# Decay rows of a token mixer: spread over the partitions by DMAs from DRAM instead of one-hot matrix products

## The chip, the cores and the metric

The kernel runs on one core of one Trainium2 chip. The metric is the device time of one launch in microseconds. The kernel before takes 2029.32 us (median of 3 runs, 2028.66 to 2029.45).

## What is computed

A decoder trunk of two layers on 512 tokens of width 1024. Each layer is a gated feed-forward block, a mixer, and a second feed-forward block. The mixer runs three kinds of heads side by side on one input projection: 4 mLSTM heads, 4 retention heads and 4 gated-delta heads, and one output projection merges them. Cut to what the change touches:

```python
bcum = jnp.cumsum(fc, axis=-1)                                   # mLSTM, per head
log_w = jnp.where(causal, bcum[..., :, None] - bcum[..., None, :] + ic[..., None, :], -jnp.inf)
m_row = jnp.maximum(log_inter, jnp.max(log_w, axis=-1))
w = jnp.exp(log_w - m_row[..., None])
...
g = jnp.cumsum(ac, axis=-1)                                      # gated delta, per head
diff = g[..., :, None] - g[..., None, :]
decay = jnp.where(causal, jnp.exp(jnp.where(causal, diff, 0.0)), 0.0)
...
o = (q * exp(g)) @ S + ((q @ k.T) * decay) @ u
...
x = x + concat(y_mlstm, y_retention, y_delta) @ w_out
```

So each of the 4 mLSTM heads and 4 delta heads has one row of 512 numbers (a running maximum, or a running sum of log decays, one number a token) that must stand in all 128 partitions: it is the term that varies along the free axis, while the other varies along the partitions.

## The kernel before

Activations lie with features on the partitions and the 512 tokens along the free axis. Each weight tile of 128x1024 is split into a high and a low part (`wh`, `wl`), and each product of 128x128 by 128x512 is made of three (`mm3`). In a mixer the input projection is 32 weight tiles of 24 products each (`pin`, in `dense_tok` `ptok`), then 8 tiles of the output projection (`po_`). The raw weights are loaded by SP's queue. The low part is made in a mixer by ScalarE (`wl` <- minus the raw tile) and a DMA of the GpSimd queue that loads the raw tile a second time and adds it (`w_split`, L299).

The small work of the heads is written as generators (`gate_math` L874, `decays` L1049, `delta_inverse` L1077, `q_post` L1208, `mlstm` L1363, and others). While the program is built, `dense_mm` and the output projection call `poll()` (L836) after each three products; it runs the next piece of a generator if a planner (`Clock`, L103) believes that its inputs are there (`mark`/`wait`) and that its engines are not too far behind (`STEPS` names the engines of each piece). So the planner's times set where each small instruction stands between the dense products. Each engine then runs its instructions in that order, whatever the true times are. `until(...)` (L850) lets the planner's time pass until a key is marked; nothing dense is put on TensorE meanwhile.

The names that matter: `prow` (rows transposed into PSUM), `RB` (the 8 rows as a high and a low part on partitions 0 to 7 and 32 to 39), `SEL` (one-hot columns), `pG` and `pM` (a row in all partitions, in PSUM), `X` and `L` (decays and products of the delta inverse), `PT` (decays times scores for the delta output), `w` (for an mLSTM pair: decays `Es`, state, scaled queries), `pP` (delta scores q k), `po` (delta output, four blocks of 128 tokens), `vb` (that output, normalised), `py` (its transposes), `g`, `yh`, `yl` (the gated result and its two parts, the right side of `po_`). The tail of a mixer runs in this sequence: `q_post` of four heads, `chain_out` (L1297, `po`), `chain_norm` (L1313, four times a reduction and a chain of small vector instructions), `merge_delta` (L1531, `py`, `g`, `yh`, `yl`). The output projection's first two tiles need only the mLSTM and retention results (48 products with `ym` and `yr`). From the third on it needs all four token blocks of the delta result (`OUT_KEYS`, L31).

Every instruction is issued from the wrapper's line L182, so the rows of the profile are told apart by their tiles.

Of the kernel before, what the change touches and what calls it, by code (L numbers as in the profile page):

```python
# [9 lines left out]
F32 = mybir.dt.float32  # L10
# [17 lines left out]
BACKLOG = 1.65  # L28
VFIRST = 0.3
WARM = 11  # L30
OUT_KEYS = [("s0",), ("s1",), ("s2",), ("s3",)] + 4 * [("s4", "s5", "s6", "s7")]  # L31
# [12 lines left out]
    gate_act="A".split(),  # L44
    gate_math="V A V VG V V A V V A".split(),
    head_norm="c V c V V G".split(),
# [3 lines left out]
    norm_cols="V A".split(),  # L50
    q_post="A VA A VG".split(),
    retention="VG Vc c".split(),
# [11 lines left out]

C_ID, C_TRI, C_ONE, C_MT, C_MS, C_M32, C_COS, C_SIN, C_HALF, C_SEL, C_DEC, C_QD, C_KD, C_GC, C_SUM, C_END = (
    0, 128, 256, 260, 388, 516, 580, 708, 836, 838, 846, 1358, 1614, 1618, 1620, 1636)

# [5 lines left out]
def const_table():  # L73
# [13 lines left out]
    c[:, C_HALF + 1] = r % 2 == 1  # L87
    for j in range(8):
        c[j, C_SEL + j] = c[32 + j, C_SEL + j] = 1.0

# [77 lines left out]
def trunk(ctx, tc, a, out):  # L168
# [100 lines left out]
    Z4 = cst.tile([4, 1], F32, name="Z4")  # L269
    SEL = cst.tile([P, 8], F32, name="SEL")  # L270
    RB = cst.tile([P, S], F32, name="RB")
    zero = cst.tile([P, 1], F32, name="zero")

# [494 lines left out]
    def mixer(l, n, nxt, after):  # L768
# [93 lines left out]

        def bcast_row(ps, j):
            m = ps.shape[0]
            T.matmul(ps, r(SEL[:, j:j + 1].broadcast_to([P, m])), r(RB), start=True, stop=True)

# [7 lines left out]
        def gate_math():  # L874
# [72 lines left out]
            for t in range(NT):  # L947
                T.transpose(prow[0:8, t * P:(t + 1) * P], ag3[:, t, :], ident)
            row = tm[6][0:8, 0:S]
            V.tensor_copy(row, prow[0:8, :])  # L950
            V.tensor_tensor_scan(row[0:4, :], Z4.broadcast_to([4, S]), prow[0:4, :], 0.0, ALU.add, ALU.max)
            yield
            A.copy(r(RB[0:8, :]), row)
            yield
            V.tensor_sub(r(RB[32:40, :]), row, RB[0:8, :])
            env.update(bg3=bg3, ag3=ag3, ng3=ng3, bt=bt)
            mark("rows")
            yield
# [3 lines left out]
            flo = COL("flo", 16)  # L962
            V.tensor_tensor(v3(flo, 4), v3(pmc[:, 0:16], 4), bg3[:, :, 0:4], ALU.add)
            yield
            A.activation(flo, flo, AF.Exp, scale=-1.0)
# [83 lines left out]
        def decays():  # L1049

            yield from wait("rows")
            bg3 = env["bg3"]
            for hd in range(4):
                pG = SM("pG")
                bcast_row(pG, 4 + hd)
                E = X[:, hd, :]
                V.tensor_tensor(v3(E, P), bc4(maskS), v3(pG, P), ALU.subtract)
                V.tensor_copy(gl[:, hd * 4:hd * 4 + 4], v3(pG, P)[:, :, P - 1])
                yield
                for t in range(NT):  # L1060
                    s = slice(t * P, (t + 1) * P)
                    A.activation(E[:, s], E[:, s], AF.Exp, bias=bg3[:, t, 4 + hd:5 + hd])
                if hd == 3:
                    mark("decays")
                yield
            bght = bg3[:, :, 4:8].rearrange("p t h -> p h t")
            V.tensor_tensor(v3(kdec, 4), v3(gl, 4), bght, ALU.subtract)
            yield
            A.activation(kdec, kdec, AF.Exp)
            A.activation(eglast, gl, AF.Exp)  # L1070
            eg = COL("eg", 16)
            A.activation(v3(eg, 4), bght, AF.Exp)
            env["eg"] = eg
            mark("eg")
            yield
# [132 lines left out]
        def q_post(hd, kT, qT, odd):  # L1208
# [9 lines left out]
            V.tensor_reduce(ssq[:, hd * 4:hd * 4 + 4], v3(PT[:, hd, :], P), AX.X, ALU.add)  # L1218
            pG = SM("pG")
            bcast_row(pG, 4 + hd)  # L1220
            V.tensor_tensor(v3(PT[:, hd, :], P), v3(pG, P), bc4(maskT), ALU.add)
            A.activation(eG, pG, AF.Exp)
            yield
# [139 lines left out]
        def mlstm(pair, mqk, V1):  # L1363
# [6 lines left out]
            for b in range(2):  # L1370
                pM = SM("pM")
                bcast_row(pM, h0 + b)
                V.tensor_tensor(v3(Es[b], P), bc4(maskT), v3(pM, P), ALU.subtract)
                hb = slice(64 * b, 64 * b + 64)
                V.tensor_copy(mc[:, 4 * b:4 * b + 4], v3(pM, P)[:, :, P - 1])
                V.tensor_copy(mp[hb, :], mc[hb, 4 * b:4 * b + 4])
                V.tensor_tensor(v3(qs[hb, :], P), bc(mp[hb, 0:3], P), v3(pM[hb, :], P)[:, 1:4, :], ALU.subtract)
                yield
                for t in range(NT):
                    c = slice(t * P, (t + 1) * P)  # L1380
                    A.activation(Es[b][:, c], Es[b][:, c], AF.Exp, bias=ag3[:, t, h0 + b:h0 + b + 1])
                yield
# [338 lines left out]
    G.memset(Z4, 0.0)  # L1721
    G.memset(zero, 0.0)
    sqs = {}
# [23 lines left out]
    n.todo += [step for p in range(4) for step in n.sums(p)]  # L1747
    n.todo.append(lambda: (A.copy(r(SEL), C[:, C_SEL:C_SEL + 8]), A.copy(r(RB), zero.broadcast_to([P, S]))))
    for l in range(DEPTH):
# [75 lines left out]
```

## Time and profile before

| | |
|---|---|
| time, median of 3 runs | 2029.32 us |
| the profiled execution's own time | 2026.25 us |
| its span, from the first to the last instruction | 2024.5 us |
| mean granted TensorE clock | 0.996 of full speed |
| busy share of PE, DVE, ACT, POOL | 98%, 70%, 53%, 13% |
| mixers in the span, about | 368 to 666 us and 1365 to 1662 us |

Times below are from the profiled execution, in us from the start of its span. TensorE (PE) is in order, and a matmul's duration there contains an overlap with the next, so what a matmul costs is the distance from one start to the next. Idle time of an engine other than PE costs nothing unless PE waits for its result.

### The profile page before, as it was taken

Reading aid. Unit: us, or ns where it says so; the run is one execution under the profiler, and the core shown is the slowest. Engines: PE = TensorE matmul, PEld = TensorE weight load, DVE = VectorE, ACT = ScalarE, POOL = GpSimd, SP = SyncE. Lnnn points to the kernel's source line nnn. Section 1 sums busy time; section 2 is a strip of 40 time slices with the busy share of each in tenths; the row PEclk is TensorE's granted clock in tenths of the full one; section 3 lists DMA queues with packets and bytes.
Section 4 is the critical chain, followed back from the end, with each engine's and each line's share of the span. In section 5 each row is a group of like instructions: output and inputs, shape, how many; then the busy total and the mean of one; then the engine's idle time right before and its main releaser. Section 6 shows DMA issues by size and latency. Waiting matters only on the chain.

```text
span 2024.5 us, 32377 instructions
## 1 busy us (share of the span) xinstructions
PE 1992.9 (98%) x12865; PEld 1765.9 (87%) x12865; DVE 1412.9 (70%) x2447; ACT 1077.3 (53%) x1607; POOL 268.9 (13%) x311
## 2 busy tenths in 40 slices
PE   9999999999999999999999999999999999999997
PEld 6999988787888899998889998877878889999886
DVE  6888934568676788883588887335777758888623
ACT  5666622564476566662365555227545756655521
POOL 0000001134212100000010000013132120000000
PEclk9999999999999999999999999999999999999999
DMA  5555422664457466633256663237734655565231
GB/s 191 156 158 161 110 96 91 174 167 105 97 116 187 122 162 162 164 99 108 94 142 158 159 160 109 86 101 176 168 84 104 150 148 151 157 157 157 90 109 50
DMA packets 77928, 270.18 MB, mean 133 GB/s; under 512 B 8912, under 2 KB 11216, under 8 KB 77776
## 3 DMA queue, kind: packets, MB, share of 16 engines
q1 hardware_dynamic: 54080, 184.73, 25.6%
q0 software_dynamic: 22608, 82.32, 24.3%
q8 instruction: 101, 1.65, 0.3%
q10 hardware_dynamic: 1088, 1.05, 0.1%
q14 instruction: 51, 0.42, 0.1%
HBM read 265.97 MB, written 2.10 MB: 132 GB/s over the span
## 4 chain that ended last, share of the span: by engine, by line
PE 90%; DVE 5%; issue 2%; DMA 1%; ACT 1%; SPq 0%; POOL 0%; DVEq 0%; ACTq 0%; POOLq 0%
PE pd L182 22%; PE px L182 16%; PE pin L182 12%; PE pz L182 11%; PE py L182 11%; PE ptok L182 3%; PE pu L182 3%; PE pg L182 2%; DVE X L182 1%; PE pav L182 1%; DVE wl L182 1%; DMA wl<-win 1%; PE po L182 1%; PE ptr L182 1%; DMA m<-wgt 1%
## 5 line engine op out<-in xcount | busy, mean ns | idle before, releaser
L182 PE MATMUL pd<-hid,wh 128*128 128x512 f32 (+1 forms) x1320 | 403.9, 388 | 1.1 <-ACT wh L182 1.1
L182 ACT CAST wh<-wr 128x512 fp32r<-128x512 f32 (+2 forms) x392 | 308.3, 809 | 11.7 <-DMA wr<-w1gu 5.4
L182 DVE TENSOR_TENSOR wl<-wr,wh 128x1024 fp32r<-128x1024 f32 (+2 forms) x276 | 279.1, 1048 | 42.5 <-ACT wh L182 42.2
L182 PEld LDWEIGHTS pd<-hid,wh 128*128 128x128 f32 x1320 | 246.3, 189 | 55.2 <-ACT wh L182 1.3
L182 PE MATMUL pd<-hid,wl 128*128 128x512 f32 (+1 forms) x660 | 255.8, 388 | 0.8 <-DVE wl L182 0.8
L182 PE MATMUL px<-ub,wh 128*128 128x256 f32 x1264 | 232.6, 282 | 1.4 <-DVE g L182 1.4
L182 PE MATMUL py<-ub,wh 128*128 128x256 f32 x1264 | 229.2, 282 | 2.3 <-ACT wh L182 2.3
L182 ACT ACTIVATE g<-g 128x512 f32<-128x512 f32 x96 | 60.5, 632 | 283.7 <-DVE g L182 283.7
L182 DVE TENSOR_TENSOR wl<-s,wh 128x1024 fp32r<-128x1024 f32 x158 | 193.1, 1222 | 12.6 <-ACT wh L182 9.9
L182 PEld LDWEIGHTS py<-ub,wh 128*128 128x128 f32 x1264 | 194.3, 189 | 2.7 <-ACT wh L182 2.7
L182 PEld LDWEIGHTS px<-ub,wh 128*128 128x128 f32 x1264 | 193.8, 188 | 2.5 <-DVE g L182 2.2
L182 PE MATMUL py<-ub,wl 128*128 128x256 f32 x632 | 177.8, 281 | 1.5 <-DVE wl L182 1.5
L182 PE MATMUL pz<-xl,wh 128*128 128x256 f32 x632 | 178.1, 282 | 0.0
L182 ACT ACTIVATE xh<-h,prm 128x512 fp32r<-128x512 f32 x48 | 34.6, 722 | 269.4 <-DVE h L182 268.9
L182 PE MATMUL pz<-xh,wh 128*128 128x256 f32 x632 | 177.6, 281 | 0.0
L182 PE MATMUL px<-ub,wl 128*128 128x256 f32 x632 | 177.5, 281 | 0.0
L182 DVE SCALAR_TENSOR_TENSOR d<-pd,rb 128x512 f32<-128x512 f32 (+1 forms) x33 | 22.3, 675 | 222.3 <-PE pd L182 222.3
L182 PE MATMUL pz<-xh,wl 128*128 128x256 f32 x632 | 177.2, 280 | 0.0
L182 ACT CAST wh<-s 128x1024 fp32r<-128x1024 f32 x158 | 164.7, 1042 | 0.0
L182 PE MATMUL pin<-xh,wh 128*128 128x512 f32 x384 | 161.2, 420 | 0.0
L182 PE MATMUL pin<-xh,wl 128*128 128x512 f32 x384 | 151.3, 394 | 2.5 <-DMA wl<-win 2.5
L182 PE MATMUL pin<-xl,wh 128*128 128x512 f32 x384 | 151.2, 394 | 0.0
(602 smaller groups left out, 4363.4 us busy)
## 6 DMA issues: line engine op xcount, KB each, us to landing
wr<-w2gu SPq DMA_DIRECT2D x88, 512.0 KB, 5.7
wr<-w1gu SPq DMA_DIRECT2D x86, 512.0 KB, 5.6
wr<-win SPq DMA_DIRECT2D x64, 512.0 KB, 4.9
wl<-win POOLq DMA_DIRECT2D x62, 512.0 KB, 6.5
s<-w2gu POOLq DMA_DIRECT2D x40, 512.0 KB, 5.7
s<-w1gu POOLq DMA_DIRECT2D x39, 512.0 KB, 5.7
wr<-w1d SPq DMA_DIRECT2D x32, 512.0 KB, 4.4
wr<-w2d SPq DMA_DIRECT2D x32, 512.0 KB, 4.3
```

Of the source, the lines that this page charges most:

```text
L182: i = f(*a_, **k_)
```

## The change

A mixer's 8 rows are kept in a tile `ROWS`, and a DMA that ScalarE issues stores them once to a DRAM tile `drows` (16 KB). Where the kernel before made a product with a one-hot column, the GpSimd queue now issues a DMA that reads one row 128 times, 2 KB into each partition (256 KB). It writes into the SBUF tile in which the result is computed anyway (`X`, `PT`, `Es`), and VectorE and ScalarE work in place on it, where they read PSUM before. The two instructions that made `RB` (a copy on ScalarE, a subtraction on VectorE), and its clearing and that of `SEL`'s copy at the start, go. Two numbers enter the planner: `BOUNCE`, the us after which it takes the rows to lie in DRAM, and `LAND`, those after which it takes a spread row to have landed. There are 12 such DMAs in a mixer: 4 at once in `decays`, 2 at once for each of the two mLSTM pairs, and one for each of 4 heads in `q_post`. The constants table's one-hot columns go too.

```diff
+LAND, BOUNCE = 5.0, 4.0
...
-    gate_math="V A V VG V V A V V A".split(),
+    gate_math="V A V VG V V VA A".split(),
...
-    q_post="A VA A VG".split(),
+    q_post="A V VA A VG".split(),
...
-    SEL = cst.tile([P, 8], F32, name="SEL")
-    RB = cst.tile([P, S], F32, name="RB")
-    zero = cst.tile([P, 1], F32, name="zero")
+    ROWS = cst.tile([8, S], F32, name="ROWS")
+    drm = ctx.enter_context(tc.tile_pool(name="drm", bufs=2, space=bass.MemoryType.DRAM))
...
-        def bcast_row(ps, j):
-            m = ps.shape[0]
-            T.matmul(ps, r(SEL[:, j:j + 1].broadcast_to([P, m])), r(RB), start=True, stop=True)
+        def spread(dst, j, key):
+
+            G.dma_start(out=dst, in_=env["drows"][j:j + 1, :].broadcast_to([P, S]))
+            marks[key] = ck_.t + LAND
...
-            row = tm[6][0:8, 0:S]
+            row = ROWS
             V.tensor_copy(row, prow[0:8, :])
             V.tensor_tensor_scan(row[0:4, :], Z4.broadcast_to([4, S]), prow[0:4, :], 0.0, ALU.add, ALU.max)
-            yield
-            A.copy(r(RB[0:8, :]), row)
-            yield
-            V.tensor_sub(r(RB[32:40, :]), row, RB[0:8, :])
             env.update(bg3=bg3, ag3=ag3, ng3=ng3, bt=bt)
-            mark("rows")
             yield
...
             V.tensor_tensor(v3(flo, 4), v3(pmc[:, 0:16], 4), bg3[:, :, 0:4], ALU.add)
+            drows = env["drows"] = drm.tile([8, S], F32, name=nm("drows"), tag="drows")
+            nc.scalar.dma_start(out=drows, in_=row)
+            marks["rows"] = ck_.t + BOUNCE
             yield
...
             for hd in range(4):
-                pG = SM("pG")
-                bcast_row(pG, 4 + hd)
+                spread(X[:, hd, :], 4 + hd, f"g{hd}")
+            for hd in range(4):
+                yield from wait(f"g{hd}")
                 E = X[:, hd, :]
-                V.tensor_tensor(v3(E, P), bc4(maskS), v3(pG, P), ALU.subtract)
-                V.tensor_copy(gl[:, hd * 4:hd * 4 + 4], v3(pG, P)[:, :, P - 1])
+                V.tensor_copy(gl[:, hd * 4:hd * 4 + 4], v3(E, P)[:, :, P - 1])
+                V.tensor_tensor(v3(E, P), bc4(maskS), v3(E, P), ALU.subtract)
...
             V.tensor_reduce(ssq[:, hd * 4:hd * 4 + 4], v3(PT[:, hd, :], P), AX.X, ALU.add)
-            pG = SM("pG")
-            bcast_row(pG, 4 + hd)
-            V.tensor_tensor(v3(PT[:, hd, :], P), v3(pG, P), bc4(maskT), ALU.add)
-            A.activation(eG, pG, AF.Exp)
+            spread(PT[:, hd, :], 4 + hd, f"G{hd}")
+            yield from wait(f"G{hd}")
+            A.activation(eG, PT[:, hd, :], AF.Exp)
+            V.tensor_tensor(v3(PT[:, hd, :], P), v3(PT[:, hd, :], P), bc4(maskT), ALU.add)
...
             for b in range(2):
-                pM = SM("pM")
-                bcast_row(pM, h0 + b)
-                V.tensor_tensor(v3(Es[b], P), bc4(maskT), v3(pM, P), ALU.subtract)
+                spread(Es[b], h0 + b, f"M{h0 + b}")
+            for b in range(2):
+                yield from wait(f"M{h0 + b}")
+                pM = Es[b]
...
                 V.tensor_tensor(v3(qs[hb, :], P), bc(mp[hb, 0:3], P), v3(pM[hb, :], P)[:, 1:4, :], ALU.subtract)
+                V.tensor_tensor(v3(Es[b], P), bc4(maskT), v3(pM, P), ALU.subtract)
...
-    n.todo.append(lambda: (A.copy(r(SEL), C[:, C_SEL:C_SEL + 8]), A.copy(r(RB), zero.broadcast_to([P, S]))))
```

Since the planner's times change, the order changes. On TensorE, where the decays are made in the first mixer (`pL` are products of the delta keys, `pG` the row products, `pin` the input projection), before:

```order
L182 MATMUL pin_3904<-xl_196,wh_3797 128x512
L182 MATMUL pin_3904<-xh_194,wl_3798 128x512
L182 MATMUL pL_3945<-kT_3589 128x128 x4
L182 MATMUL pG_3951<-RB,SEL 128x512
L182 MATMUL pin_3904<-xh_194,wh_3797 128x512
L182 MATMUL pin_3904<-xl_196,wh_3797 128x512
L182 MATMUL pin_3904<-xh_194,wl_3798 128x512
L182 MATMUL pin_3965<-xh_193,wh_3859 128x512
```

and with the change:

```order
L181 MATMUL pin_3860<-xh_193,wl_3728 128x512
L181 MATMUL pL_3909<-kT_3586 128x128 x4
L181 MATMUL pin_3915<-xh_192,wh_3794 128x512
L181 MATMUL pin_3915<-xl_194,wh_3794 128x512
L181 MATMUL pin_3915<-xh_192,wl_3795 128x512
L181 MATMUL pin_3915<-xh_192,wh_3794 128x512
```

The row products are gone there; the dense products on both sides are the same, and the `pL` stand 21 to 24 dense products earlier.

On POOL, at the end of the first mLSTM pair (`R` is work of the rotary embedding for retention, `vb` a value convolution, `wl` the low parts of weights), before:

```order
L182 TENSOR_TENSOR R_4264<-rx_4262,C 128x8x32 x2
L182 TENSOR_TENSOR R_4264<-R_4264 128x8x32
L182 MEMSET m_3576 128x3
L182 TENSOR_TENSOR R_4264<-R_4264,C 128x256
L182 DMA wl_4652<-win 128x1024
L182 TENSOR_TENSOR R_4264<-rx_4262,C 128x8x32 x2
L182 TENSOR_TENSOR R_4264<-R_4264 128x8x32
L182 TENSOR_TENSOR vb_4544<-vb_4544 128x512
L182 TENSOR_TENSOR R_4264<-R_4264,C 128x256
```

and with the change:

```order
L181 TENSOR_TENSOR R_4259<-rx_4257,C 128x8x32 x2
L181 TENSOR_TENSOR R_4259<-R_4259 128x8x32
L181 MEMSET m_3573 128x3
L181 DMA wl_4596<-win 128x1024
L181 TENSOR_TENSOR R_4259<-R_4259,C 128x256
L181 DMA w_515_3581<-drows_3883 128x512 x2
L181 TENSOR_TENSOR vb_4505<-vb_4505 128x512
L181 TENSOR_TENSOR R_4259<-rx_4257,C 128x8x32 x2
L181 TENSOR_TENSOR R_4259<-R_4259 128x8x32
```

The second pair's two rows (into `w`) stand behind a weight load and ahead of the convolution's addition and the next turn of the rotary embedding. The first of the two waits for TensorE to be done with the first pair's `w`.

On TensorE at the tail of the first mixer (`py` with `vb` are the transposes of the last block of the delta result; `po_` with `ym` or `yr` need nothing of it, and `po_` with `yh` or `yl` need all of it), before:

```order
L182 MATMUL po__824_5999<-ym_5605,wh_5856 128x512 x2
L182 MATMUL po__824_5999<-ym_5605,wl_5857 128x512
L182 MATMUL py_6003<-C,vb_4544 128x128 x4
L182 MATMUL py_6009<-C,rqk_4263 128x128 x4
L182 MATMUL po__824_5999<-ym_5605,wh_5856 128x512 x2
L182 MATMUL po__824_5999<-ym_5605,wl_5857 128x512
...
L182 MATMUL po__827_6019<-yr_5944,wh_5916 128x512 x2
L182 MATMUL po__827_6019<-yr_5944,wl_5917 128x512
L182 MATMUL po__822_5980<-yh_5812,wh_5976 128x512
L182 MATMUL po__822_5980<-yl_5813,wh_5976 128x512
```

and with the change:

```order
L181 MATMUL po__810_5957<-yr_5888,wh_5819 128x512 x2
L181 MATMUL po__810_5957<-yr_5888,wl_5820 128x512
L181 MATMUL py_6035<-C,vb_4505 128x128 x4
L181 MATMUL po__810_5957<-yr_5888,wh_5819 128x512 x2
L181 MATMUL po__810_5957<-yr_5888,wl_5820 128x512
L181 MATMUL po__807_5930<-yh_5880,wh_5926 128x512
L181 MATMUL po__807_5930<-yl_5881,wh_5926 128x512
L181 MATMUL po__807_5930<-yh_5880,wl_5927 128x512
```

Between the last `py` and the first product with `yh` there stand 33 dense products before (most of them left out here) and 3 with the change. The last head's scores `pP` stand 156 dense products ahead of that first product before, and 93 with the change.

## Rows read from the trace of the kernel before

**Rows 1.** The profile's page: busy time by engine, share, instructions.
```profile
PE 1992.9 (98%) x12865; PEld 1765.9 (87%) x12865; DVE 1412.9 (70%) x2447; ACT 1077.3 (53%) x1607; POOL 268.9 (13%) x311
```
**Rows 2.** Busy us by engine in one stretch of the first mixer; clock; DMA.
```profile
560.00:640.00 80.00, 79.42 (x420) 67.04 (x419) 50.39 (x133) 51.85 (x79) 14.38 (x15) 1.00 0.66 151
```
**Rows 3.** Tiles pG and pM: the row products, whole run, duration ns min/median/max.
```profile
L182 PE MATMUL pG<-RB,SEL x16: 389/476/500, 399.2 to 1576.9; 128*128 128x512 f32 x16
L182 PE MATMUL pM<-RB,SEL x8: 392/393/482, 442.8 to 1474.0; 128*128 128x512 f32 x8
```
**Rows 4.** Chain that ended last, first mixer: start us, us, what.
```profile
410.27 0.23 PE pG L182
...
600.60 1.78 PE po L182 x16
602.39 10.38 PE pin L182 x45
```
**Rows 5.** What PE waited for, 340 to 680 us: us in total, times, longest.
```profile
PE pin L182 <- DMA wl<-win: 1.5, 1, 1.5
PE ptr L182 <- ACT vb L182: 1.0, 1, 1.0
PE pSm L182 <- DVE w L182: 0.6, 1, 0.6
PE pS L182 <- DVE vb L182: 0.6, 1, 0.6
PE prt L182 <- POOL R L182: 0.6, 1, 0.6
```
**Rows 6.** DMA issues: tiles, queue, count, size, median us from issue to landing.
```profile
wl<-win POOLq DMA_DIRECT2D x62, 512.0 KB, 6.5
wr<-w1d SPq DMA_DIRECT2D x32, 512.0 KB, 4.4
wl<-wo POOLq DMA_DIRECT2D x16, 512.0 KB, 8.2
wr<-w1d SPq DMA_DIRECT2D x16, 384.0 KB, 3.1
out<-h ACTq DMA_DIRECT2D x4, 256.0 KB, 2.5
```
**Rows 7.** ACT in order of time: start us, us, what.
```profile
481.90 1.27 ACT L182 ACTIVATE w<-w,ag 128x128 f32<-128x128 f32 x4
487.15 1.28 ACT L182 ACT_TABLE_LOAD   x1
488.44 0.63 ACT L182 ACTIVATE vb<-vb 128x512 f32<-128x512 f32 x1
```
**Rows 8.** POOL in order of time: start us, us, what.
```profile
405.23 0.86 POOL L182 DMA_DIRECT2D wl<-win  x1 [8.47 <-ACT wl L182]
```
**Rows 9.** DVE at the tail of the first mixer, in order of time.
```profile
587.98 0.69 DVE L182 TENSOR_TENSOR PT<-pP,PT 128x512 f32<-128x512 f32 x1 [0.20 <-ACT PT L182]
589.78 0.16 DVE L182 TENSOR_SCALAR ssq<-ssq 128x16 f32<-128x16 f32 x1
592.37 0.68 DVE L182 TENSOR_TENSOR g<-pin,rb 128x512 f32<-128x512 f32 x1
593.60 0.69 DVE L182 TENSOR_REDUCE sso<-m 128x4 f32<-128x512 f32 x1 [0.21 <-ACT m L182]
597.58 0.42 DVE L182 CAST wh<-wr 128x512 fp32r<-128x512 f32 x1
624.62 0.69 DVE L182 TENSOR_TENSOR g<-py,g 128x512 f32<-128x512 f32 x1 [1.38 <-PE py L182]
626.00 0.69 DVE L182 TENSOR_TENSOR yl<-g,yh 128x512 fp32r<-128x512 f32 x1
```
**Rows 10.** Tile yh in the tail: the first product with it; ns, first and last start.
```profile
L182 ACT CAST yh<-g x4: 620/622/622, 614.0 to 625.3; 128x512 fp32r<-128x512 f32 x4
L182 PE MATMUL po__822_5980<-yh,wh x4: 393/393/393, 632.5 to 638.7; 128*128 128x512 f32 x4
```

More of the change, by code (lines that the diff above doesn't have):

```diff
@@ L62 @@
 O_GQ, O_GK, O_GV, O_GZ, O_GA = 2056, 2568, 3080, 3592, 4104
-C_ID, C_TRI, C_ONE, C_MT, C_MS, C_M32, C_COS, C_SIN, C_HALF, C_SEL, C_DEC, C_QD, C_KD, C_GC, C_SUM, C_END = (
-    0, 128, 256, 260, 388, 516, 580, 708, 836, 838, 846, 1358, 1614, 1618, 1620, 1636)
+C_ID, C_TRI, C_ONE, C_MT, C_MS, C_M32, C_COS, C_SIN, C_HALF, C_DEC, C_QD, C_KD, C_GC, C_SUM, C_END = (
+    0, 128, 256, 260, 388, 516, 580, 708, 836, 846, 1358, 1614, 1618, 1620, 1636)
 Q_N1, Q_NM, Q_N2, Q_MG, Q_RG, Q_GG, Q_CONV, Q_BIAS, Q_ALOG = 0, 8, 16, 24, 26, 28, 32, 80, 96
@@ L87, in const_table @@
     c[:, C_HALF + 1] = r % 2 == 1
-    for j in range(8):
-        c[j, C_SEL + j] = c[32 + j, C_SEL + j] = 1.0
     lg = np.log1p(-np.exp2(-5.0 - np.arange(4)))
@@ L1721, in trunk @@
     G.memset(Z4, 0.0)
-    G.memset(zero, 0.0)
     sqs = {}
```

## The prediction

> **What bounds the kernel now.** I read the page's busy times first: TensorE is busy 98% of the span [rows 1]. Then a stretch of the mixer by itself: 79.42 of 80 us, at a granted clock of 1.00, with VectorE and ScalarE at 63 and 65% [rows 2]. Then the chain that ended last. Inside the mixer it is one piece of TensorE after another, and it gives prices on TensorE: 45 dense products take 10.38 us, so 0.231 us each; 16 small ones 1.78 us, so 0.111 us each; a row product 0.23 to 0.24 us [rows 4]. Last, what TensorE itself waited for in the first mixer: the five largest waits are 1.5, 1.0, 0.6, 0.6 and 0.6 us [rows 5]. So whatever leaves TensorE shortens the time, and whatever is put behind a result that comes later than TensorE gets to it lengthens it. The other engines matter only through such results.
>
> **What is removed.** There are 24 row products in the run, 16 `pG` and 8 `pM` [rows 3]. Their 389 to 500 ns overlap with the neighbours; by the chain each costs 0.23 us [rows 4]. All stand between dense products, on the path: 24 x 0.23 = 5.5 us less. ScalarE's and VectorE's two instructions on `RB` a mixer go too; they are off the path, worth nothing.
>
> **What is added off the path.** POOL issues 12 more DMAs a mixer at 0.86 us of its time each [rows 8], 10 us of a mixer in which it is mostly idle (14.4 of 80 us busy in [rows 2]). The bytes: 12 x 256 KB is six weight tiles' worth (512 KB) beside the mixer's 80 or so, at a DMA share of 0.66 [rows 2]; I cost it at nothing while a low part still lands before its use. The cover is that weights are split two tiles ahead (`weights` queues tile i + 2): 2 x 24 x 0.231 = 11 us against the 6.5 us of landing [rows 6], so 4.6 us, and a burst of four holds POOL for 3.4. If it were gone, each tile after a burst would wait for what is over 4.6 us. ScalarE gets about four more table loads a mixer at 1.28 us [rows 7]; it has a third of its time free. The vector and scalar instructions on the rows are as many as before.
>
> **How long a spread takes to land.** No row shows a read of one DRAM row into 128 partitions. From below: on SP's queue 512 KB land in 4.4 and 384 KB in 3.1 us, 256 KB on ScalarE's queue in 2.5 [rows 6]. From above: the POOL queue's adding loads of 512 KB land in 6.5, in the crowded tail 8.2 us [rows 6]. I take 3.2 us, near the 256 KB row, with something for the POOL queue; ends 2.4 and 8.2. The store of the 16 KB ahead is taken like the 2.5 us store of 256 KB. Here a rule of the Trainium skill can be weighed (DMA: Bandwidth & Descriptors, section Anatomy of one DMA): a software-queue DMA takes about 2.0 us plus its bytes at 436 GB/s, 2.6 us for 256 KB by its fit, and it warns that completion is slowest where HBM is written. The 256 KB store in 2.5 us agrees with it; POOL's adding loads of 512 KB, 6.5 us, are far above its 3.2. With 2.6 us for a spread instead of my 3.2 the sum below would be about 1 us smaller.
>
> **Where the waits are added.** In `decays` POOL's four spreads wait for the stored rows; a low part of a weight is behind them, with the 4.6 us of cover. The exponentials of the fourth head end about when they did, and VectorE's next step waits for the key projection's last tile anyway. Nothing there. For the second mLSTM pair the two spreads wait until TensorE is done with the first pair's tile. Behind them in POOL are a convolution's addition and the rotary embedding; in ScalarE's queue, behind the exponentials that need the spread, a table load and the convolution's activation `vb` (1.27, 1.28, 0.63 us [rows 7]), whose transposes TensorE reaches 27 dense products after the first pair's outputs. From those outputs to there TensorE has 27 x 0.231 = 6.2, plus 12 transposes, 8 more and some 40 smaller products, about 6: 12.2 us. The other side: about 2 us of copies and a weight part on ScalarE, two issues and a small step on POOL (2.2), landing, 1.5 on VectorE, 1.27 + 1.28 + 0.63, and handoffs of a tenth or two: 9.5 us plus the landing. With 3.2 us TensorE waits 0.5 us; it waited 1.0 us there before [rows 5]. Each us of landing beyond costs one.
>
> **What is moved.** The order is dealt anew over some 250 us of each mixer. Three old waits lose their place: the transposed rotary rows (`prt`) now stand 20 dense products apart instead of 9, the state product `pSm` 18 instead of 12 behind its input, and `pS` has two groups of outputs ahead of it. That is 0.6 + 0.6 + 0.6, and with the half us at `vb` 2.3 us a mixer, 4.6 in two. A new order has waits of its own that I can't name; bounds are none and as much as all of rows 5 again; I take half of what goes, so -2.2 us in all.
>
> The tail is the heavy part. The last head's scores `pP` stand 156 dense products before the first product that needs `yh`; with the change 93, since each head in `q_post` now waits for a landing and two heads follow one another on a lane. Before, the last `yl` is done at 626.7 us [rows 9] and first wanted at 632.5 [rows 10]: 5.8 us to spare. The 63 products are worth 14.6 us, so the spare is gone. Counted from the start of the last `pP`:
> - TensorE gets to the first `yh` after 93 x 0.231 = 21.5 us and 56 small products (28 `po`, 24 `py`, 4 `pP`) x 0.111 = 6.2; `yl` is wanted 0.2 later: 27.9 us.
> - VectorE: the scores' product is done at 1.3. The first block's square is there at 5.3 (`po`, a copy, the square). Each of four blocks takes 597.58 - 593.60 = 4.0 us, reduction to product [rows 9], 16.0 together (VectorE's 2.6 us for the norm of q, 589.78 to 592.37, pass in the first 5.3). Between the blocks the order puts a cast, a square, two gate evacuations, two products with `py` and two subtractions at 0.6 to 0.7 us of distance: 4.8. That is 26.1. After the fourth block VectorE still has eight instructions: five at 0.6 (3.2), one `yl` behind ScalarE's copy (1.4; the copy alone is 0.62 [rows 10]), and the last `g` to `yl`, 624.62 to 626.69 [rows 9], 2.1. Together 32.8.
>
> So TensorE waits 4.9 us for it, in each mixer. Nothing dense is left to put there: the input projection is over and the 48 products that don't need the delta result stand ahead. Twice 4.8, rounded down for what I may have put on VectorE twice, is 9.6 us. Bounds: at least 2.1 - 0.9 = 1.2 us a mixer (the last `g` to `yl` against three products and the 0.2), at most 7, if ScalarE's weight part and casts between the last two `yh` are in the way.
>
> **Sum.** -5.5 - 2.2 + 9.6 = +1.9 us on the profiled execution's 2026.25 us: 2028.2. That execution is 3.1 us under the median of the runs, 2029.3, which the change moves alike: 2031.2 us. A measurement of this kernel tells 0.2%, about 4 us, from no change; +1.9 is within.
>
> **Rivals.** Slower: the spreads land late and the tail is at its upper end. Each spread reads the same 2 KB 128 times; if that is served like the adding loads, landing is 6.5 to 8.2 us. Place: `vb` behind the second pair's exponentials, plus 3.3 to 5 us a mixer; with the tail at 6 instead of 4.8, that is +1.9 + 2 x (3.3 + 1.2) = +11, 2040 us. It is slower than 0.2% from a landing of 4.3 us on, or from a tail of 5.9 us, either alone. For it: POOL's rows in the tail, 8.2 us, and that small vector instructions wait for one another with nothing spare. Against it: 256 KB in 2.5 us, and no adding.
>
> Faster: the tail is nearly covered. If VectorE has part of its work between the blocks done earlier, or the fourth `pP` comes sooner than its place says, the floor of 1.2 us a mixer stays: -5.5 - 2.2 + 2.4 = -5.3, 2024.0 us; with no new waits 2022. For it: TensorE's part is sure, and the planner that set the order means the results to be there. Against: its bill above leaves 4.9 us out.
>
> That the change doesn't do what it says is ruled out by the order: the row products are gone, and the dense ones are the same number.
>
> **Chances.** The forecast, within 0.2%: 0.44. Slower: 0.37, since each of its two causes is enough. Faster: 0.19. The likeliest case's own range is 2026 to 2033; low end of the whole 2023.0 (the faster rival less a us), high end 2040.0.
>
> **What would show it.** Right: no `pG` and `pM` rows; a wait of TensorE of 4 to 6 us at the first `po_` with `yh`, put down to `yl` or `yh`, in both mixers; spreads landing in about 3 us; the stretch up to the last input projection tile 3 to 4 us shorter a mixer. Wrong: no such wait, then the time is 2024 or less; or waits at `ptr` for `vb` of more than 1 us, then landing was mis-sized. A weight part (`wl`) that TensorE waits for in the middle of a mixer would mean that the queue's cover was not there.

## The result, and the profile after

The changed kernel takes 2049.14 us (median of 4 runs, 2045.14 to 2051.96), the kernel before 2028.99 us beside it (2028.36 to 2029.45): ratio 1.0097, 95% interval 1.0083 to 1.011. It is slower, by 20 us, and the time lies above the range. The profiled execution took 2051.96 us, 2.8 over this median, and its span is 2050.2 us; that of the kernel before was 2.7 under its own, so the profiles lie further apart than the runs.

The page's busy row, against [rows 1]: 24 products fewer, and TensorE is busy 7 us more.

```profile
PE 1999.9 (98%) x12841; PEld 1770.1 (86%) x12841; DVE 1407.5 (69%) x2441; ACT 1088.2 (53%) x1615; POOL 283.4 (14%) x334
```

By stretches the loss has two places. I cut each mixer at the last product of the input projection (`pin`): the front runs from the gate rows (`pgr`) to there, the tail from there to the first product of the next feed-forward part. Front: 251.9 us before, 257.1 after; tail: 45.8 before, 54.0 after (means of the two mixers; they differ by 0.4 us at most). Twice 5.2 and twice 8.2 are 26.8 us; the spans differ by 25.7. The stretches of the first mixer with the loss, columns as in [rows 2], before:

```profile
460.00:500.00 40.00, 37.21 (x352) 29.09 (x353) 34.74 (x80) 22.30 (x43) 17.07 (x22) 1.00 0.44 99
620.00:660.00 40.00, 40.00 (x182) 32.76 (x181) 22.76 (x34) 25.42 (x40) 10.27 (x10) 1.00 0.72 181
```

and after; the last is the one that [rows 2] shows, with 79.42 us of TensorE and a clock of 1.00:

```profile
460.00:500.00 40.00, 33.72 (x234) 27.09 (x231) 25.53 (x59) 18.48 (x33) 13.05 (x20) 0.83 0.36 88
620.00:660.00 40.00, 34.99 (x161) 27.91 (x160) 24.65 (x68) 20.29 (x33) 5.31 (x5) 0.96 0.54 127
...
560.00:640.00 80.00, 75.12 (x403) 63.19 (x402) 52.52 (x143) 53.37 (x85) 19.09 (x21) 0.98 0.68 155
```

TensorE stands for 6 us between 460 and 500 us, and its granted clock is 0.83 there. What it waited for from 340 to 700 us, against [rows 5]:

```profile
PE po__807_5930 L181 <- ACT yr L181: 3.8, 1, 3.8
PE prt L181 <- DVE R L181: 3.3, 1, 3.3
PE pSm L181 <- DVE w L181: 3.0, 1, 3.0
PE pin L181 <- DMA wl<-win: 2.1, 2, 1.3
PE po__807_5930 L181 <- ACT yh L181: 0.7, 1, 0.7
...
PE po__807_5930 L181 <- DVE yl L181: 0.2, 1, 0.2
PE po__807_5930 L181 <- DVE yr L181: 0.2, 1, 0.2
```

The wait at `ptr` for `vb` is gone; `prt` and `pSm`, which were to lose their 0.6 us, have 3.3 and 3.0; the tail waits at `yr` first. Behind these waits TensorE works at half speed: here at `prt`, in order of time, two dense products start 0.42 us apart (493.33 and 493.75) where 0.23 is usual. The records of the granted clock have a stretch at its lower level, 1.2 GHz, from 490.3 to 497.1 us here, from 469.8 to 476.6 at `pSm` and from 637.0 to 640.4 behind `yr`; in the kernel before the mixers have none.

```profile
492.02 1.09 PE L181 MATMUL prt<-C,R 128*128 128x128 f32 x4 [3.30 <-DVE R L181]
...
493.33 0.63 PE L181 MATMUL pin<-xl,wh 128*128 128x512 f32 x1
493.75 0.63 PE L181 MATMUL pin<-xh,wl 128*128 128x512 f32 x1
```

`prt` waits for the rotary step `R`, and that stands on VectorE behind a row: the copy `mc` waits for the second pair's spread, and the rotary step comes five instructions later.

```profile
488.80 0.17 DVE L181 COPY mc<-w 128x4 f32<-128x4 f32 x1 [5.34 <-DMA w<-drows]
...
490.67 0.75 DVE L181 TENSOR_TENSOR R<-rx,C 128x256 f32<-128x256 f32 x2
```

The DMA issues, as in [rows 6]:

```profile
wl<-win POOLq DMA_DIRECT2D x62, 512.0 KB, 6.7
...
X<-drows POOLq DMA_DIRECT2D x8, 256.0 KB, 6.3
w<-drows POOLq DMA_DIRECT2D x8, 256.0 KB, 6.9
PT<-drows POOLq DMA_DIRECT2D x8, 256.0 KB, 6.0
```

As a median a spread lands in 6.0 to 6.9 us, not in 3.2. GpSimd in order of time shows what stands ahead of it on its queue: an adding load of a weight part (`wl`), issued 0.6 to 2.1 us before at these three places.

```profile
480.84 0.88 POOL L181 DMA_DIRECT2D wl<-win  x1 [11.58 <-DVE X L181]
481.46 0.92 POOL L181 TENSOR_TENSOR R<-R,C 128x256 f32<-128x256 f32 x1
482.02 1.43 POOL L181 DMA_DIRECT2D w<-drows  x2
...
549.39 0.89 POOL L181 DMA_DIRECT2D wl<-win  x1 [9.95 <-ACT qT L181]
549.98 0.88 POOL L181 DMA_DIRECT2D PT<-drows  x1
...
593.33 0.86 POOL L181 DMA_DIRECT2D wl<-win  x1 [6.03 <-ACT wl L181]
...
595.41 0.62 POOL L181 DMA_DIRECT2D PT<-drows  x1
```

The packets that the DMA engines recorded agree. The spread issued at 482.0 us has its first packet 3.5 us later, when the adding load ahead of it is nearly done (its last packet ends 3.8 us after that issue); one that no load stands ahead of has its first packet after 1.3 to 1.7 us. Of the 24 spreads 22 began 2.6 to 5.1 us after their issue. Once they run, their packets of 4096 bytes take 159 ns as a median, as SyncE's weight packets of that size do; the adding loads' take 328. So reading one row 128 times is not slow; standing behind an adding load on the same queue is.

### The profile page after: what moved, and what is told of

Read it like the earlier page. It is cut to its first block, busy times and chain, and to the rows that moved or that the text cites. A ratio compares the mean times of both kernels' runs of the same rounds, so it can differ in the third digit from the quotient of the medians.

```text
span 2050.2 us, 32368 instructions
## 1 busy us (share of the span) xinstructions
PE 1999.9 (98%) x12841; PEld 1770.1 (86%) x12841; DVE 1407.5 (69%) x2441; ACT 1088.2 (53%) x1615; POOL 283.4 (14%) x334
## 4 chain that ended last, share of the span: by engine, by line
PE 84%; DVE 5%; DMA 4%; issue 4%; ACT 2%; POOL 1%; SPq 0%; DVEq 0%; ACTq 0%; POOLq 0%
PE pd L181 21%; PE px L181 16%; PE pz L181 11%; PE py L181 11%; PE pin L181 9%; PE ptok L181 4%; PE pg L181 2%; PE pu L181 2%; DMA wl<-win 2%; DVE wl L181 1%; PE pav L181 1%; DMA w<-drows 1%; DMA PT<-drows 1%; ACT wh L181 1%; PE pt L181 1%
## 5 line engine op out<-in xcount | busy, mean ns | idle before, releaser
L181 ACT CAST wh<-wr 128x1024 fp32r<-128x1024 f32 (+2 forms) x394 | 309.5, 808 | 10.0 <-DMA wr<-w1gu 5.5
```

The source lines that it names most:

```text
L181: i = f(*a_, **k_)
```

## The experiments

A table ahead, in us: the median of the runs, its ratio to the kernel before on the same chip with the 95% interval, and front and tail of a mixer in the profiled execution (means of two).

| kernel | median | ratio | front | tail |
|---|---|---|---|---|
| before | 2029.0 | | 251.9 | 45.8 |
| changed | 2049.1 | 1.0097 [1.0083, 1.011] | 257.1 | 54.0 |
| E1 order, products | 2042.2 | 1.0064 [1.0047, 1.0081] | 253.6 | 53.8 |
| E2 planned for 7 us | 2044.5 | 1.0073 [1.0053, 1.0094] | 252.1 | 53.8 |
| E3 SyncE's queue | 2037.6 | 1.0042 [1.0027, 1.0057] | 250.2 | 54.1 |
| E4 filler | 2046.8 | 1.0085 [1.0066, 1.0103] | 255.6 | 53.5 |
| E5 q by products | 2054.0 | 1.0113 [1.0095, 1.013] | 264.9 | 45.9 |
| E6 only q by spreads | 2024.4 | 0.9973 [0.9961, 0.9984] | 249.6 | 47.8 |
| E7 q's spreads early | 2029.8 | 1.0013 [0.9999, 1.0027] | 253.4 | 45.6 |
| E8 E7 on SyncE's queue | 2024.2 | 0.9966 [0.995, 0.9983] | 253.0 | 45.6 |
| E9 filler, moved | 2040.1 | 1.0058 [1.0041, 1.0074] | 252.7 | 52.4 |
| E10 decays only | 2040.5 | 1.0053 [1.0038, 1.0068] | 259.3 | 45.4 |
| E11 mLSTM only | 2055.9 | 1.0131 [1.0116, 1.0146] | 266.7 | 46.8 |
| E12 E6, spreads early | 2024.6 | 0.998 [0.9969, 0.999] | 250.4 | 46.7 |

**E1. The order alone.** The edit, for the decays (the other two places likewise; `RB` and `SEL` are made again):

```diff
-            G.dma_start(out=dst, in_=env["drows"][j:j + 1, :].broadcast_to([P, S]))
             marks[key] = ck_.t + LAND
...
+                pG = product(4 + hd)
-                V.tensor_copy(gl[...], v3(E, P)[:, :, P - 1])
+                V.tensor_copy(gl[...], v3(pG, P)[:, :, P - 1])
```

> The changed kernel with every instruction in its place, but the rows come from products again: each of the 24 products stands on TensorE where the first use of its spread stands, and nothing is stored or spread. The planner still counts 5 us of landing, so its order is the same. Theory L (landing): TensorE's waits at pSm and prt, about 3.3 us each a mixer, come from spreads that land in 6 to 7 us; without them both fall under 1 us, and the stretches at half clock behind them go. The waits of the tail stay, since they are of the order. 2049 - 2 x (6.5 + 4) + 5.5 = 2033 us. Rival O (order): the order that a landing of 5 us makes puts results behind their use whatever brings the rows; both waits stay and the products come on top: 2049 + 5.5 = 2054 us. What this kernel differs from before is then the price of the order alone.

Measured: 2042.2 us, between the two. TensorE's longest waits in the whole run:

```profile
PE pSm L183 <- DVE w L183: 5.2, 2, 3.0
PE po__2159_15716 L183 <- ACT yr L183: 3.8, 1, 3.8
PE po__818_5945 L183 <- ACT yr L183: 3.8, 1, 3.8
```

`prt` is off the list: that wait was the landing's. `pSm` keeps 2.6 of its 3.3 us a mixer and the tail all of its length: those are the order's. The new order by itself costs 8.0 us a mixer in the tail and 1.7 in front. The front of the changed kernel is another 3.5 us longer although it has 12 products less, which are 12 x 0.23 = 2.8 us: landings cost it 6.3 us a mixer. By the runs the order alone is 12.6 us over the kernel before beside it (2029.6 us).

**E2. A landing of 7 us in the plan.** `LAND, BOUNCE = 7.0, 4.0` for `5.0, 4.0`.

> The changed kernel with one number changed: the planner counts 7 us of landing instead of 5, nearer to the 6.0 to 6.9 us measured. Theory L: steps behind a spread are put later, vector and scalar engine no longer stand still for a row with other work behind it; the waits at pSm and prt fall under 1 us each, and the time to 2032 to 2040 us; the tail's wait may grow, since each q head takes 2 us more. Rival O: a new order has new waits of the same size at other places, 2044 to 2054 us.

Measured: 2044.5 us (2039.5 to 2048.55). `pSm` is covered, and other waits came, nearly as the rival had it:

```profile
PE prt L181 <- DVE R L181: 5.7, 2, 3.0
PE ptr L181 <- DVE Tm L181: 5.4, 2, 3.1
PE po__2137_15690 L181 <- ACT yr L181: 3.5, 1, 3.5
```

A truer number in the planner is worth 5 us a mixer in front by the profiles and nothing in the tail; by the medians it is 4.6 us in all, with runs of both kernels that overlap.

**E3. Another queue.** `nc.sync.dma_start` for `G.dma_start` in `spread`; the order is the same.

> The changed kernel with the 12 spreads of a mixer issued on SyncE's queue instead of GpSimd's, everything else in the same order. Theory Q (queue): GpSimd's software queue is what makes 256 KB take 6 us; on SyncE's they land in 2.5 to 3.5 us, the waits at pSm and prt fall under 1 us, the time to 2028 to 2036 us. Rival R (row): 128 reads of one 2 KB row are slow on any queue; they land in 5.5 to 7 us and the time stays at 2046 to 2052 us. A weight load that stands behind a waiting spread on SyncE would show as a wait for wr.

Measured: 2037.6 us, 11.6 under the changed kernel, and between the two theories; the landings:

```profile
w<-drows SPq DMA_DIRECT2D x8, 256.0 KB, 4.0
X<-drows SPq DMA_DIRECT2D x8, 256.0 KB, 9.8
PT<-drows SPq DMA_DIRECT2D x8, 256.0 KB, 5.0
```

The second pair's spreads also leave earlier:

```profile
473.99 1.79 SPq L863 DMA_DIRECT2D w<-drows  x2
```

That is as the first pair's last output product that reads the tile (`pav`, to 474.2 us, an end that is modelled) is done. In the changed kernel its `pav` with that tile ends at 477.7 and GpSimd issues at 482.02, since a weight's load and a rotary step stand ahead on that engine (rows above): 4.3 us later, and 2.9 us more to land. The wait at `prt` is 0.3 us a mixer now. Against E1, with the compute engines in the same order, E3's front is 3.4 us shorter; the 12 products saved are 2.8 of that. `X` lands later than on GpSimd's queue, in 9.8 us, four of 256 KB issued within 2.9 us with the first pair's two just ahead. VectorE waits for it 7.8 us at most where it was 5.5, and `pSm` keeps the 2.6 us a mixer that E1 has:

```profile
DVE gl L181 <- DMA X<-drows: 14.7, 2, 7.8
...
PE pSm L181 <- DVE w L181: 5.2, 2, 3.0
```

So the longer stand for `X` costs nothing at `pSm`. What the other queue gives back, 11.6 us in all, comes mostly from the second pair's landing: the wait at `prt` (3.2 us a mixer) and the half clock behind it. The tail is none of its doing.

**E4 and E9. Filler for the clock.** Products of constants that are thrown away, at the three places of long waits; E9 moves those of the tail.

```diff
             pS = SM("pSm")
+            if pair == 0:
+                fill(pS, 12)
...
                 pr_ = SM("prt")
+                if t == 1:
+                    fill(pr_, 13)
...
                 until(*OUT_KEYS[k])
+                if k == 2 and d == 0:      # E9: k == 3
+                    fill(psm.tile(...), 15)
```

> The changed kernel with products of constants, 128x512 in bfloat16, put on TensorE at the three places where it waits in each mixer: 12 ahead of the first pair's pSm, 13 ahead of the second block of prt, 15 ahead of the first output product with yr. Their results are thrown away. At 0.22 us each they fill 2.6, 2.9 and 3.3 us of waits of 3.0, 3.3 and 3.8 us. Theory C (clock): the stretches at half clock behind these waits go, and with them what the granted clock shows of them: 3.4, 5.1 and 3.4 us of work at half speed a mixer, half of which is lost, 6 us a mixer: 2049 - 12 = 2037 us. Rival: the clock falls for another reason than idle TensorE, or the products only lengthen the waits: 2049 to 2053 us, half-clock stretches as before.

> As the run with filler products, but the 15 of the tail stand directly ahead of the product that waits for yr (the second feature block of yr), instead of 6 products earlier. So TensorE has 2.6, 2.9 and 3.3 us of thrown-away products inside its three waits of a mixer and nothing else is changed. Theory C (clock): no half-clock stretch is left in the mixers; what comes back is half of the work done at half clock in the changed kernel, 1.7 + 2.5 + 1.7 us a mixer: 2049 - 12 = 2037 us. Rival: the half clock behind a wait costs little, since TensorE waits again soon after for results that come no earlier: 2044 to 2050 us.

Measured: E4 2046.8 us. Its tail products ran ahead of the wait, not in it, and 1.7 us of wait stayed behind them; but by the table that is 1.1 us a mixer against E9, and 2.9 are in front, where the order is the same. There E4's profile has stretches at half clock at the start of both mixers (372.2 to 379.1 us in the first), behind a wait of 1.4 us for a weight; E9 has a wait of 1.25 us there and no such stretch. E9 2040.1 us, 9.0 under the changed kernel (12 expected); in its profile both mixers are 6 us shorter. The 12 left work out: in the two mixers of the changed kernel TensorE works 6.0 and 3.1 us at half clock behind `pSm`, 5.1 and 6.6 behind `prt` and 3.4 behind `yr`, half of which is 13.8 us in all. The stretches that stand above for the changed kernel, here at full clock:

```profile
460.00:500.00 40.00, 39.13 (x302) 29.13 (x303) 26.99 (x63) 22.55 (x41) 18.08 (x26) 1.00 0.40 95
620.00:660.00 40.00, 38.18 (x171) 29.04 (x171) 26.64 (x56) 23.36 (x38) 9.25 (x9) 1.00 0.58 131
```

Nothing but the thrown-away products was added, and the half clock behind the waits is gone, so what comes back is the clock: of the loss of 20 us some 9 to 12 are work at half speed behind waits.

**E5. q by products, the rest by spreads.** In `q_post` the four lines from `spread` to the exponential are those of the kernel before again, with `SEL` and `RB`.

> The changed kernel, but the four q heads of a mixer take their rows from products with one-hot columns again (8 products in the run); the decays and both mLSTM pairs keep their spreads. The order is planned anew: 192 dense products stand between the last head's scores pP and the first product with yh, where the changed kernel has 93 and the kernel before 156. Theory T (tail by q_post): the 8 us a mixer that the tail lost are the price of the four landings in q_post; TensorE has no wait over 1 us behind the last input projection, and the time is 2049 - 16 + 2 = 2035 us, less if fewer transfers let the spreads in front land sooner. Rival F (front): the tail is late because the mixer's front is late (pSm, prt); the tail keeps its wait of 4 us at yr and the time stays at 2046 or more.

Measured: 2054.0 us. The tail is back at 45.9 us, as theory T had it, and the time is not: the order planned anew makes the front 13 us longer than before, with waits of up to 4.3 us at `pz` and 1.6 at `prt`.

```profile
PE pz L183 <- DVE m L183: 8.3, 2, 4.3
PE prt L183 <- DVE R L183: 7.0, 6, 1.6
```

**E6. Spreads in q alone.** The reverse: decays and pairs by products as in the kernel before, `q_post` as in the changed one.

> The kernel before, but with the spreads in q_post alone; decays and mLSTM pairs keep their 16 products. 150 dense products stand between the last pP and the first product with yh (156 before, 93 in the changed kernel). Theory T: any landing in q_post costs the tail; the wait at yr or yh comes back with 3 to 5 us a mixer, 2036 to 2042 us. Theory D (distance): only the distance in dense products decides; at 150 the tail has its 5.8 us to spare less 1.4, no wait, 8 products less: 2029 - 1.8 = 2027 us, up to 2030 with small new waits.

Measured: 2024.4 us, 0.3% faster than before. A landing in `q_post` costs the tail less than theory T had it: at 150 dense products it waits 1.1 us. The distance alone doesn't set that wait either (E12 below has 144 and waits 0.4). And the same DMAs on the same queue now land in 3.8 us as a median: in 3.3 to 3.7 for the first two heads of a mixer, with no load just ahead, and in 3.9 to 5.6 for the other two:

```profile
549.02 0.61 POOL L183 DMA_DIRECT2D PT<-drows  x1 [1.04 <-DVE ssq L183]
549.62 0.12 POOL L183 MEMSET m<- 128x3 f32 x1
550.87 0.86 POOL L183 DMA_DIRECT2D wl<-win  x1 [1.13 <-ACT wl L183]
...
PT<-drows POOLq DMA_DIRECT2D x8, 256.0 KB, 3.8
```

**E7, E8 and E12. All four q spreads at once, early.**

```diff
                 env["PT"] = U("PT")
+                for j in range(4):
+                    spread(PT[:, j, :], 4 + j, f"G{j}")
...
-            A.activation(PT[:, hd, :], ps, AF.Square)
+            A.activation(eG, ps, AF.Square)
```

E7 is the changed kernel with that, E8 also has SyncE's queue, E12 is E6 with it.

> The changed kernel, but the spreads of all four q heads are issued together when their tile is taken, ahead of the first head's transposes; the squares of q, which had used that tile, go to the tile of the exponentials. No head waits for a landing of its own; 159 dense products stand between the last pP and the first product with yh. Theory D: the tail's 8 us a mixer come back, the front stays as it is: 2049 - 16 = 2033 us. Rival: the landings still hold the heads or four spreads at once hold the weights (waits of pin for wl of 2 us and more): 2040 to 2049 us.

> As the run with the q heads' spreads issued together, and all spreads of the mixer on SyncE's queue instead of GpSimd's, in the same order. If the tail (8 us a mixer) and the queue (11.6 us in all, 2049.1 less 2037.6) are two causes that add up, 2037.6 - 16.2 = 2021 us, under the kernel before by the products and the three old waits. If the four spreads together hold up the weight loads behind them on SyncE (waits for wr or wl over 1 us), 2026 to 2032 us.

> Spreads in q_post alone, on GpSimd's queue, and all four of a mixer issued together when their tile is taken; decays and pairs by products. 144 dense products between the last pP and the first with yh (150 with a spread in each head's turn, 156 before). With no tail wait it is 2024.4 us, the time of the run with spreads in q_post alone, or a microsecond less, since no vector or scalar step stands for a landing; with the distance at 144, 1.4 us less to spare than at 150, a wait of up to 1 us a mixer at yr or yh could come: 2026 us.

Measured: 2029.8, 2024.2 and 2024.6 us. With 159 products of distance the tail is 45.6 us in E7 and E8: no wait there at all. E7 is level with the kernel before; in front it keeps 3.1 us a mixer at `prt`. E8 is under it, with 2.2 at `pSm`; the sum expected was 3 us lower. E12 is no better than E6, with 0.4 us of wait in its tail, and its spreads, now behind a weight's load, land in 8.7 us with nothing waiting for them.

**E10 and E11. One part of the front alone.** Decays by spreads, all else by products; then the mLSTM pairs.

> The kernel before with the spreads in the decays alone (4 a mixer, 8 products less in the run), order planned anew; the last pP stands 171 dense products ahead of the first with yh, so no tail. Theory W (work behind a row): in the changed kernel VectorE stood 5.3 us at the first gl copy for X's landing, everything behind it came later, and TensorE waited 3.3 us at pSm with half clock behind. Here that wait of VectorE is still there, and pSm waits 2 to 4 us: 2029 - 2 + 2 x 4 = 2035 us. Rival: the wait for X is covered, as the prediction had it, and the spreads of the mLSTM pairs made the front late: 2026 to 2029 us.

> The kernel before with the spreads in the two mLSTM pairs alone (4 a mixer, 8 products less), order planned anew; 153 dense products between the last pP and the first with yh, so no tail. Theory W: the second pair's spreads land 6 to 7 us after their issue, behind an adding load of a weight on the same queue; VectorE stands for them with the rotary step and vb behind it, TensorE waits 3 us or more at prt (or ptr for vb) with half clock behind: 2029 - 2 + 2 x 5 = 2037 us. Rival: the wait was made by the decays' delay in front of it, and the pairs alone cost nothing: 2026 to 2030 us.

Measured: 2040.5 and 2055.9 us; slower both times, as theory W had it, and the pairs far beyond it. What VectorE waited for in the run, decays first, and TensorE behind it:

```profile
DVE gl L183 <- DMA X<-drows: 19.1, 2, 9.6
...
PE pSm L183 <- DVE w L183: 6.1, 2, 3.1
```

```profile
DVE mc L183 <- DMA w<-drows: 31.1, 4, 9.1
...
PE pSm L183 <- DVE X L183: 15.4, 2, 7.9
PE prt L183 <- DVE R L183: 12.2, 2, 6.3
```

For the decays that doesn't show the cause: E1 waits 2.6 us a mixer at `pSm` with no landing at all, and E3 the same with VectorE standing 7.8 us at `gl`, so the 3.1 us here may be the order planned anew. For the pairs it is seen in order of time on VectorE: the small steps of the triangular inverse (`X`) stand still for 7.3 us in their middle, behind a copy that needs a row.

```profile
439.78 4.04 DVE L183 TENSOR_TENSOR X<-X 128x96 f32<-128x96 f32 x10
451.13 0.17 DVE L183 COPY mc<-w 128x4 f32<-128x4 f32 x1 [7.30 <-DMA w<-drows]
...
452.72 3.48 DVE L183 TENSOR_TENSOR X<-X 128x133 f32<-128x133 f32 x8
```

The three parts alone, against the kernel before: -5 us (q), +12 (decays), +27 (pairs). They don't add up to the 20 of all three, since each has an order of its own.

## Why the prediction was wrong

**The sum beside the runs.** The sum had -5.5 us for the products, +7.4 for the new order (-2.2 and +9.6) and nothing for landings. E1 keeps the products and has no landing, so its 12.6 us over the kernel before are the order's. The changed kernel is 20.1 us over the one beside it, 7.5 more, with 5.5 us of products gone: landings cost about 13 us, by these medians. So two terms failed, the landing by 13 us and the order by 5; and no term had the clock, which is in both.

**What was right.** The products leave TensorE, at about 0.23 us each: E3's front is 3.4 us shorter than E1's in the same order, where 12 products make 2.8. E3's profile also has 3.4 us less at half clock in each front, so this bears the price out only roughly.

**The tail, 4.8 against 8.2 us.** It is all the order's: E1 has 8.0 without a landing. The wait was forecast as 4.8 us a mixer, and the four rows of the tail above are 3.8 + 0.2 + 0.7 + 0.2 = 4.9, but that is luck. The wait is at `yr`, whose gate stands on VectorE behind the fourth block's norm, and only then at `yh`; and both sides of the comparison were too short. On TensorE I counted 28 `po` and 4 `pP` of a mixer at the 0.111 us of [rows 4], but that is the price of a record, and each of these products is two records in the trace. Here are the 112 records of the 56 `po` in both mixers of the kernel before:

```profile
L182 PE MATMUL po<-vb,PT x64: 270/275/275, 590.4 to 1598.3; 128*128 128x128 f32 x64
L182 PE MATMUL po<-m,qT x48: 270/275/275, 592.7 to 1598.0; 128*128 128x128 f32 x48
```

That is 32 x 0.111 = 3.6 us more on TensorE, with which the sum would have had a wait of 1.3 us. VectorE's side was too short as well: its last products with `py` wait 2.2 and 2.3 us for transposes that stand on TensorE behind the wait at `yr`. From the last `pP` to the first product with `yh` it is 38.2 us in the changed kernel (607.1 to 645.3), where the sum had 32.8. The tail's other 3.3 us are 1.6 of work lost to the 3.4 us at half clock behind `yr`, 0.4 for four `py` more behind the last `pin`, and 1.3 that I can't account for. The upper bound of 7 had no clock in it.

**The landing, 3.2 against 6.0 to 6.9 us.** The step that failed is the reading of [rows 6]: I put the rows of plain transfers and of adding loads down to their kind, and priced the queue only for what stands *behind* a spread (the weight's cover of 4.6 us). What stands *ahead* of it counts: E6 has 3.3 to 3.7 us for the same DMA with no load just ahead, so 3.2 was nearly right for a case that the changed kernel hardly has. GpSimd's two issues were counted, the 4.3 us that they stand behind its other work were not. The Trainium skill says, of the queues of SyncE and ScalarE, that each DMA engine takes descriptors in the order of its ring (DMA: Bandwidth & Descriptors, section Queues, rings and completion order). The packets above show GpSimd's queue doing the same. The fit of 2.6 us that I weighed is not reached even with no load just ahead (3.3 us), and the 2.5 us store that I held beside it runs on ScalarE's queue, not on GpSimd's.

**Half a us behind the second pair, and "nothing" in `decays`.** Behind the waiting row I listed GpSimd's and ScalarE's queues, and of VectorE's nothing but the row's own 1.5 us. But the row's first user is a copy on VectorE, and that engine stood 5.3 us at `mc`, with the rotary step behind it. The wait came at `prt`, not at `ptr`: 3.5 us a mixer where 0.6 was. It is the landing's, for E1 has none there and E3 0.3. In `decays` VectorE stood as long, at `gl`, but there "nothing" comes out nearly right: the wait at `pSm` is 3.3 us a mixer in the changed kernel and 2.6 in E1 without a landing, and E3 keeps it at 2.6 with the longer stand. So `pSm` is mostly the new order's, which I had as a gain: half of the old waits was to go (-2.2 us in all). With the old ones gone and 2.8 us of products saved, the front should have been 3.8 us shorter and is 5.2 longer: 9 us a mixer, the larger part of the miss.

**No term for the clock.** Every wait was costed at its length. By E9 what the long waits take from the work behind them is 4.5 to 6 us a mixer (half of 9.0 by the runs, of 12 by the mixers of the profile), more than any one of the waits.

**The rivals.** The slower one had about the landing's size (6.5 to 8.2 us) and not its cause: 128 reads of one row run at 159 ns a packet like any other. It also had the wrong place (`vb`), so its 2040 us would have been too low even with the right landing. That faster was possible was right of a part: rows for q alone give it (E6), and with the spreads early the whole change comes to the level of the kernel before (E7) or under it (E8).

**What stays open.** E6, E8 and E12 are 4 to 5 us under the kernel before by their runs, while their profiled spans (2022.2, 2023.9 and 2023.9 us) are no more than 2.3 us under that of the kernel before (2024.5), which was taken 2.7 us under its median; so where the gain lies isn't read from the mixers. The runs of the changed kernel, E2, E4, E5, E7 and E12 lie 7 to 12 us apart, those of E1, E3, E10 and E11 1 to 2.4. In the changed kernel the spread goes with the granted clock of the run (0.992 at 2045.1 us, 0.988 or 0.989 at 2048.9 to 2052.0); what sets it is not shown. No run separates in E10 and E11 what is landing and what is order, and why the new order waits at `pSm` wasn't followed up.

## What to carry to other kernels

A transfer has the price of its queue at that moment: look at what was issued on the queue before it, not only at its bytes and at what comes after. An engine that works in order and whose next instruction needs a late result delays all that stands behind it, so a wait is priced by the first thing behind it that the bound engine needs. Where a product is cheap on the bound engine and its replacement has a latency, replace it where the result can be fetched long ahead (q's rows here), and leave it where the result is new and wanted at once.

## What was not expected of the hardware

The same DMA of 256 KB on the same queue landed in 3.3 us at best (E6) and 8.7 us as a median (E12), by what stood ahead of it. In the changed kernel waits of TensorE of 3.0 to 3.9 us were followed by 3.1 to 6.6 us of work at 1.2 instead of 2.4 GHz, while waits of up to 1.5 us in the mixers of the kernel before were followed by none; E9 removed such stretches with products whose results nobody reads. The length of the wait alone doesn't tell: 2.2 us at `pSm` was followed by such a stretch in E1 and by none in E3, and 1.0 us at `ptr` by one in E12 and by none in the kernel before.
